# Output pieces on another queue and a longer split tail in a fused mLSTM, attention and expert layer

## The chip, the cores and the metric

The kernel is one program on one core of a Trainium2 chip. The metric is the device time of one launch in microseconds (us), the median of several runs. All data are fp32; large products are made from split operands (below).

## The reference, cut to what matters

One layer on 256 tokens of width 2048. The first half (mLSTM and a sparse attention, both fed by a wide projection of the normalised input) ends in `x = x + gate1 * y`. The change touches the start (the norm), the passage from the first half to the second, and the second half, which is a product-key expert layer:

```
h2 = rmsnorm(x, norm2_g) * (1 + scale2) + shift2
q  = (h2 @ wq).reshape(n_tok, 8, 2, 128)
sc = einsum('nhpd,pkd->nhpk', q, subkeys)        # top 16 of 128 twice, then top 16 of 256
a  = einsum('td,thkd->thk', xb, u_tab[eidx])     # 16384 experts, 2048 wide
w  = softmax(top) * gelu(a)
x  = x + gate2 * einsum('thk,thkd->td', w, v_tab[eidx])
```

## The kernel before, in words

**Split products.** A weight unit is a 128 x 1024 fp32 load of 512 KB (`load_unit`, L212, on SP's queue) into one of a ring of raw buffers (`raw_slots`). ScalarE (ACT) rounds it to a high part (L217), VectorE (DVE) subtracts to get the low part (L218). `mm3` (L242 to L244) makes a product of three matmuls: high by low, high by high, low by high. SP's queue is served in order: a load whose buffer is not yet free holds back every later issue.

**Start.** `rms_bcast` squares the input in four pieces of 128 x 1024 (L452), adds them in pairs (L453) and sums over partitions on TensorE (L455). The squares go to a ring of two buffers (`w4`), so the second pair of pieces waits until the first is used up. Behind it TensorE makes the first modulation group (L392), and only then the first projection.

**Passage to the second half.** `y_phase` makes 16 column tiles of the output projection. While the last is made, `q_first` loads the two halves of the first query tile (`wq[0]`) and splits the first half only, into the buffers hl0 and hl1. Then come the norm (L985 to L989), `make_h`, which for each of 16 blocks of 128 features runs two DVE operations of 128 x 256 (L465, L468) with one on ACT between them (L467), and the eight pieces of the residual x1, transposed on TensorE (L570), copied out of PSUM by ACT into a ring of three buffers `w2` (L1001) and stored to DRAM from ACT's queue (L1002). `peer` starts by splitting the second half of `wq[0]` into buffers of a new pool, starts seven small loads from ACT's queue (L1244 to L1254: an index row, the subkeys, an identity, four bias rows), and copies the identity on ACT (L1249). Its first loop makes 16 query tiles (two units each), and loads 20 units of the modulation `wmB`, which DVE sums up (L355, L357). Instructions up to the end of this loop are ordered by the framework, by readiness; from there on `pin()` fixes the order on each engine to the order of the code.

**U stage.** For 128 steps `e` the kernel makes expert scores (L1194, L1203, L1204). From step `G0` = 58 on, 48 steps also scatter the gates of four tokens: GpSimd and ACT make two one-hot factors (L1146 to L1148), TensorE multiplies them (L1156), ACT and DVE place the result (L1159, L1162).

**V stage.** 128 experts in 256 steps (expert e, half u of 1024 columns). Each step splits one unit of V and makes ten matmuls of 512 columns into the banks of that half (`v_mm`). The eight PSUM banks hold the whole output: quarters q = 0, 1 belong to u = 0, quarters 2, 3 to u = 1. The last `NT` = 8 experts go by halves: first u = 0 of all eight, then u = 1, so quarters 0 and 1 are complete after step 247. `v_out(q)` finishes a quarter: an ACT copy (L1391), five DVE operations (L1392 to L1397) and two stores of 256 KB (L1394, L1398), here on SP's queue. Before, `v_out(0)` stands behind step 251, `v_out(1)` behind step 252, and quarters 2 and 3 after the last step. In steps 252 to 255 only quarter 2's matmuls are made; quarter 3's follow at the end.

Of the kernel before, what the change touches and what calls it, by code (L numbers as in the profile page):

```python
# [12 lines left out]
AF = mybir.ActivationFunctionType  # L13
# [5 lines left out]
T = 256  # L19
# [3 lines left out]
TD = 192  # L23
# [3 lines left out]
C_ONE, C_MS, C_MT, C_QA, C_KA, C_CA, C_CM, C_VD = 0, 128, 256, 384, 448, 452, 454, 484  # L27
# [110 lines left out]
class Kernel:  # L138
# [307 lines left out]
    def rms_bcast(self):  # L446
        nc = self.nc
        ps = self.bank()
        for j in range(2):
            sq, s2 = self.w4(), self.w4()  # L450
            for i, t in enumerate((sq, s2)):
                nc.scalar.activation(t, self.xT[:, 8 * j + 4 * i:8 * j + 4 * i + 4, :], AF.Square)  # L452
            nc.vector.tensor_tensor(sq, sq, s2, op=ALU.add)  # L453
            for i in range(4):
                nc.tensor.matmul(ps[:, :T], self.cst[:, C_ONE:C_ONE + 128], sq[:, i * T:i * T + T], start=(j + i == 0), stop=(j == 1 and i == 3))  # L455
        r = self.wk.tile([128, T], F32, tag="rbc", name=self.nm("rbc"), bufs=1)
        nc.scalar.activation(r, ps[:, :T], AF.Sqrt, bias=self.eps, scale=1.0)
        nc.vector.reciprocal(r, r)
        return r
# [482 lines left out]
        return pc  # L942

    def q_first(self):
        self.raw_slots = self.st_raws()
        self.half_slots = [(self.st, "hl0"), (self.st, "hl1")]
        s = self.a["wq"][0].rearrange("p d c -> p (d c)")
        self.q0r = [self.load_unit(s[:, c:c + 1024]) for c in (0, 1024)]
        return self.split(self.q0r[0])

    def proj_mm(self, pc, kts):
        b = self.bank("z")
# [6 lines left out]
    def y_phase(self):  # L959
        nc = self.nc  # L960
        self.load_x()
        nxt = self.proj_load(self.a["wo"][0], (1, 0))
        self.hmix()
        kts = list(range(8, 16)) + list(range(0, 8))
        sq = self.wk.tile([128, T], F32, tag="sqs", name="sqs", bufs=1)
        for ct in range(16):
# [3 lines left out]
            pc = nxt  # L970
            nxt = self.proj_load(self.a["wo"][ct + 1], (1, 0)) if ct < 15 else self.q_first()
            b = self.proj_mm(pc, kts)
# [3 lines left out]
            else:  # L976
                s = self.w1()
# [6 lines left out]
        ps = self.bank()  # L984
        nc.tensor.matmul(ps[:, :T], self.cst[:, C_ONE:C_ONE + 128], sq, start=True, stop=False)  # L985
        nc.tensor.matmul(ps[:, :T], self.cst[:, C_ONE:C_ONE + 128], s, start=False, stop=True)
        r = self.wk.tile([128, T], F32, tag="rbc", name=self.nm("rbc"), bufs=1)
# [7 lines left out]
        for tt in range(2):  # L995
            for q in range(4):
                ps = self.bank("s")
                for j in range(4):
                    self.tr(ps[:, j * 128:j * 128 + 128], self.xT[:, 4 * q + j, tt * 128:tt * 128 + 128])
                t = self.w2()  # L1000
                nc.scalar.activation(t, ps, AF.Copy)  # L1001
                nc.scalar.dma_start(self.d_x1[tt, :, 512 * q:512 * q + 512], t)  # L1002

    def topk16(self, vals, idx, src, n):
        nc, tk = self.nc, self.tk
# [219 lines left out]
    def peer(self):  # L1225
        nc, P, a = self.nc, self.pools, self.a
# [3 lines left out]
        self.tk = tk = P.open("tk")  # L1230
        self.half_slots = [(tk, "hl0"), (tk, "hl1"), (tk, "hl2"), (gp, "ug2"), (self.st, "hl0"), (self.st, "hl1")]
        self.sc = 0
        q1 = self.split(self.q0r[1])
        self.iT = um.tile([128, 4, TD], F32, name="iT")
        self.x32 = um.tile([128, 3, KF, 64], F32, name="x32")
        self.xr = gp.tile([128, D], F32, tag="xr", name="xr", bufs=1)
# [4 lines left out]
        self.ga = gp.tile([128, 64], F32, name="ga")  # L1241
        self.sk = tk.tile([128, 2, 128], F32, name="sk")
        self.iota16 = tk.tile([128, 16], F32, name="iota16")
        nc.scalar.dma_start(self.iota16, a["idio"][:, 128:144])  # L1244
        nc.scalar.dma_start(self.sk, a["sk"])
        self.ident = tk.tile([128, 128], F32, name="ident2")
        nc.scalar.dma_start(self.ident, a["idio"][:, 0:128])
        self.idr = tk.tile([128, 128], F32R, name="idr")
        nc.scalar.activation(self.idr, self.ident, AF.Copy)  # L1249
        g2t = gp.tile([128, D], F32, tag="ug0", name="g2t", bufs=1)  # L1250
        acc, rows = [g2t[:, 0:1024]], g2t[:, 1024:1024 + T]
        bg = g2t[:, 1280:1792].rearrange("p (h c) -> p h c", h=2)
        for q in range(4):
            nc.scalar.dma_start(bg[32 * q:32 * q + 1, :, :], a["bg2"].rearrange("o (h q c) -> o q h c", h=2, q=4)[:, q])  # L1254
        self.qa = tk.tile([128, 16, T], F32, name="qa")
        self.top = tk.tile([128, 2, 8, 16], F32, name="top")
        self.isel = tk.tile([128, 2, 2, 128], F32, name="isel")
        self.WB = [wba.tile([128, 64, TD], F32, name="WBa"), None]
        nxt = self.q0 + q1
        gate2 = [f for half in range(2) for f in self.mod_gate2(half, acc, rows, bg)]  # L1260
        for i in range(16):
            for f in gate2[max(i - 2, 0) * self.GQ // 14:max(i - 1, 0) * self.GQ // 14]:
                f()
            if i == self.QX:
                self.raw_slots += [(tk, "rawx0"), (tk, "rawx1"), (gp, "ug1")]
            if i in (3, 4, 5):
                x3 = self.x32[:, i - 3]
                nc.vector.tensor_tensor(x3, *(self.hx[:, i - 3, 0:KF, k, :].bitcast(F32) for k in range(2)), op=ALU.add)
            pc = nxt
            if i < 15:  # L1270
                nxt = self.proj_load(self.a["wq"][i + 1])
            else:
                n = len(self.raw_slots)
                self.fl = [self.raw_slots[(self.uc + j) % n] for j in range(n)]
                self.ul = [(1, 0), (0, 0), (1, 1)] + [p for e in range(1, 127) for p in ((0, e), (1, e + 1))] + [(0, 127), (1, 128), (1, 129)]
                self.ur = {}
                self.last = {}
                self.pinned = len(nc.cur_bb.bb.instructions)
                for j in nc.cur_bb.bb.instructions:
                    self.last[j.engine] = j.name  # L1280
                self.u_fill()
            self.q_tile(i, pc)
# [11 lines left out]
        next(tp[0])  # L1294
        ts = list(range(24)) + [25 + i * 30 // 24 for i in range(24)]
        ge = list(range(26, 58, 2)) + [58 + i * 66 // 48 for i in range(48)]
        g4 = [e for e in range(self.G0, 128) if (e - self.G0) % 5 < 4][:TD // 4]
        dots = []
        td = 0
        k = 0  # L1300
        for e in range(128):
# [9 lines left out]
            b = self.u_mm0(e)  # L1311
# [60 lines left out]
        nv = 0  # L1372
        mm = nc.tensor.matmul
        seq = list(range(64, 128)) + list(range(64))
        NT = 8
        tail = seq[-NT:]
        order = [(e, u) for e in seq[:-NT] for u in range(2)] + [(e, u) for u in range(2) for e in tail]

# [8 lines left out]

        def v_out(q):
            c = slice(512 * q, 512 * q + 512)
            o = self.raw_tile((vx, f"o{q}"))[:, 0:512]  # L1390
            nc.scalar.activation(sh[0:64, c], y[1][q][64:128, :], AF.Copy)  # L1391
            nc.vector.tensor_tensor(o, y[0][q], g2[:, c], op=ALU.mult)  # L1392
            nc.vector.tensor_tensor(o, o, x1[:, c], op=ALU.add)
            nc.sync.dma_start(a["out"][0:128, c], o)  # L1394
            nc.vector.tensor_tensor(sh[0:64, c], y[1][q][0:64, :], sh[0:64, c], op=ALU.add)
            nc.vector.tensor_tensor(sh[:, c], sh[:, c], g2[:, c], op=ALU.mult)
            nc.vector.tensor_tensor(sh[:, c], sh[:, c], x1b[:, c], op=ALU.add)  # L1397
            nc.sync.dma_start(a["out"][128:T, c], sh[:, c])  # L1398

        late = []  # L1400
        for step, (e, u) in enumerate(order):
            if step == 128:
# [25 lines left out]
            else:  # L1428
                late.append((e, pc))
                v_mm(e, u, 0, pc)  # L1430
            if step == 251:
                v_out(0)
            if step == 252:
                v_out(1)
            self.pin()
            if e == 72 and u == 1:
                hy = self.hh.tile([128, 4, D], F32, tag="hx", name="hy", bufs=1)
# [3 lines left out]
                nc.scalar.dma_start(x1b, self.d_x1[1])  # L1441
        for e, pc in late:
            v_mm(e, 1, 1, pc)
        v_out(2)
        v_out(3)
        self.pin()

    def build(self):
# [33 lines left out]
```

## Time and profile before

| | |
|---|---|
| median of 3 runs | 2049.55 us (2049.22 to 2050.61) |
| the profiled execution | 2048.65 us, span 2046.9 us |
| mean granted clock of TensorE | 0.991 |
| TensorE (PE) busy | 1971.2 us, 96% of the span |
| DVE, ACT, GpSimd (POOL) busy | 74%, 52%, 21% |
| DMA | 612.06 MB, mean 299 GB/s |

The page also shows the span in 40 slices of 51 us. PE is busy at nine tenths or more in all but the first (7) and the last (6); its granted clock is at 9 (full) in all but the last (8). In an answer of the trace, "idle before <- releaser" in brackets is the time that the engine stood still before the instruction and what ended it. SPq and ACTq are the issue of DMAs on those engines' queues.

### The profile page before, as it was taken

Reading aid. Unit: us, or ns where it says so; the run is one execution under the profiler, and the core shown is the slowest. Engines: PE = TensorE matmul, PEld = TensorE weight load, DVE = VectorE, ACT = ScalarE, POOL = GpSimd, SP = SyncE. Lnnn points to the kernel's source line nnn. Section 1 sums busy time; section 2 is a strip of 40 time slices with the busy share of each in tenths; the row PEclk is TensorE's granted clock in tenths of the full one; section 3 lists DMA queues with packets and bytes.
Section 4 is the critical chain, followed back from the end, with each engine's and each line's share of the span. In section 5 each row is a group of like instructions: output and inputs, shape, how many; then the busy total and the mean of one; then the engine's idle time right before and its main releaser. Section 6 shows DMA issues by size and latency. Waiting matters only on the chain. (4 is left out here: it accounts for less than half of the span.)

```text
span 2046.9 us, 34175 instructions
## 1 busy us (share of the span) xinstructions
PE 1971.2 (96%) x12601; PEld 1707.9 (83%) x12601; DVE 1522.9 (74%) x2695; ACT 1062.3 (52%) x2055; POOL 426.1 (21%) x359
## 2 busy tenths in 40 slices
PE   7999999999998999999999999999999999999996
PEld 6887877675898999999999999999677777777774
DVE  3777778864557669989966666676788888888885
ACT  5444336673445434333377778763455555555552
POOL 0000001001010000011166667651122221322200
PEclk9999999999999999999999999999999999999998
DMA  8877986619886878788888988888999999999972
GB/s 328 306 276 271 330 317 247 227 48 361 280 291 227 292 252 283 245 316 305 304 302 318 331 316 311 327 316 294 362 338 366 341 361 342 396 348 357 365 278 86
DMA packets 151544, 612.06 MB, mean 299 GB/s; under 512 B 17089, under 2 KB 18257, under 8 KB 134609
## 3 DMA queue, kind: packets, MB, share of 16 engines
q1 hardware_dynamic: 130320, 469.25, 64.3%
q0 software_dynamic: 18432, 134.23, 17.2%
q10 hardware_dynamic: 2624, 6.40, 0.8%
q8 instruction: 100, 1.64, 0.3%
q14 instruction: 68, 0.55, 0.1%
HBM read 605.61 MB, written 4.20 MB: 298 GB/s over the span
## 5 line engine op out<-in xcount | busy, mean ns | idle before, releaser
L217 ACT ACTIVATE hl<-raw 128x512 fp32r<-128x512 f32 (+1 forms) x601 | 483.9, 815 | 553.9 <-PE z L244 242.2
L218 DVE TENSOR_TENSOR hl<-raw,hl 128x512 fp32r<-128x512 f32 (+1 forms) x601 | 542.3, 921 | 235.3 <-ACT hl L217 234.0
L1194 PE MATMUL z<-x,raw 128*128 128x192 f32 x2048 | 353.9, 326 | 0.0
L1194 PEld LDWEIGHTS z<-x,raw 128*128 128x128 f32 x2048 | 336.9, 190 | 0.4 <-PE t L1022 0.4
L1204 PE MATMUL z<-hx 128*128 128x384 f32 x976 | 289.5, 361 | 0.0
L1203 PE MATMUL z<-hx 128*128 128x192 f32 x976 | 258.4, 265 | 0.8 <-DVE hx L218 0.8
L242 PE MATMUL z<-hx,hl 128*128 128x256 f32 x848 | 244.3, 288 | 12.0 <-DVE hx L468 10.0
L244 PE MATMUL z<-hx,hl 128*128 128x256 f32 x848 | 241.7, 286 | 2.7 <-DVE hl L218 2.6
L243 PE MATMUL z<-hx,hl 128*128 128x256 f32 x848 | 241.5, 285 | 0.0
L1093 POOL DMA_INDIRECT ug<-in_V_dram,gix x64 | 131.9, 2061 | 427.8 <-DVE yg L1116 368.5
L1203 PEld LDWEIGHTS z<-hx 128*128 128x128 f32 x976 | 186.5, 191 | 3.1 <-DVE hx L218 2.4
L1093 POOL DMA_INDIRECT ug<-in_UG_dram,gix x64 | 92.7, 1448 | 440.0 <-DVE ts L1061 249.1
L1204 PEld LDWEIGHTS z<-hx 128*128 128x128 f32 x976 | 183.5, 188 | 0.0
L242 PEld LDWEIGHTS z<-hx,hl 128*128 128x128 f32 x848 | 163.3, 193 | 23.3 <-ACT hl L217 9.3
L1146 POOL TENSOR_SCALAR e<-iota,iT 128x128 f32<-128x128 f32 x192 | 166.0, 877 | 75.2 <-PE t L1156 61.0
L218 DVE TENSOR_TENSOR hx<-raw,hx 128x1024 fp32r<-128x1024 f32 x124 | 151.4, 1221 | 25.5 <-ACT hx L217 25.5
L244 PEld LDWEIGHTS z<-hx,hl 128*128 128x128 f32 x848 | 163.0, 192 | 5.1 <-DVE hl L218 4.5
L243 PEld LDWEIGHTS z<-hx,hl 128*128 128x128 f32 x848 | 163.1, 192 | 0.3
L1116 DVE SCALAR_TENSOR_TENSOR yg<-ug,gw,yg 128x2048 f32<-128x2048 f32 x63 | 147.8, 2346 | 0.6 <-DMA ug<-in_V_dram,gix 0.6
L1208 ACT ACTIVATE c<-z 128x192 f32<-128x192 f32 x128 | 41.9, 327 | 202.6 <-PE z L1204 189.3
L1103 DVE SCALAR_TENSOR_TENSOR ug<-ug,xr 128x2048 f32<-128x2048 f32 x64 | 146.8, 2294 | 0.0
L217 ACT ACTIVATE hx<-raw 128x1024 fp32r<-128x1024 f32 x124 | 130.0, 1049 | 0.0
(384 smaller groups left out, 3615.7 us busy)
## 6 DMA issues: line engine op xcount, KB each, us to landing
raw<-in_U_dram SPq DMA_DIRECT2D x256, 512.0 KB
raw<-in_V_dram SPq DMA_DIRECT2D x256, 512.0 KB
raw<-in_wmB_dram SPq DMA_DIRECT2D x128, 512.0 KB
raw<-in_wt_dram SPq DMA_DIRECT2D x64, 512.0 KB
raw<-in_wmA_dram SPq DMA_DIRECT2D x48, 512.0 KB
raw<-in_wo_dram SPq DMA_DIRECT2D x32, 512.0 KB
raw<-in_wq_dram SPq DMA_DIRECT2D x32, 512.0 KB
raw<-in_wz_dram SPq DMA_DIRECT2D x30, 512.0 KB
```

What stands on the lines that cost most here:

```text
L217: nc.scalar.activation(hi, raw, AF.Copy)
L218: nc.vector.tensor_tensor(lo, raw, hi.bitcast(F32), op=ALU.subtract)
L242: mm(ps, sh, ml, start=first, stop=False, skip_group_check=skip)
L243: mm(ps, sh, mh, start=False, stop=False, skip_group_check=skip)
L244: mm(ps, sl, mh, start=False, stop=last, skip_group_check=skip)
L1093: self.nc.gpsimd.indirect_dma_start(out=t, out_offset=None, in_=self.a[name].rearrange("a b d -> (a b) d"), in_offset=bass.IndirectOffsetO ...
L1103: nc.vector.scalar_tensor_tensor(t, t, 1.0, self.xr, op0=ALU.mult, op1=ALU.mult, accum_out=self.ga[:, n:n + 1])
L1116: nc.vector.scalar_tensor_tensor(self.yg, t, w, self.yg, op0=ALU.mult, op1=ALU.add)
L1146: nc.gpsimd.tensor_scalar(e0, self.iota, self.iT[:, 0, t:t + 1], None, op0=ALU.is_equal)
L1194: self.nc.tensor.matmul(b[:, 0:TD], r[:, dt * 128:dt * 128 + 128], self.x32[:, :, dt, :], start=dt == 0, stop=False, skip_group_check=True)
L1203: mm(b[:, TD:2 * TD], lo[:, c], self.hx[:, 0:3, dt, 0, :], start=False, stop=False, skip_group_check=True)
L1204: mm(b[:, 0:2 * TD], hi[:, c], self.hx[:, 0:3, dt, :, :].rearrange("p b k t -> p k b t"), start=False, stop=dt == 15, skip_group_check=True)
```

## The change

Six edits. (1) `rms_bcast` squares into four separate places (of `zqk`, free at that time). (2) `q_first` loads and splits both halves of `wq[0]`; its four split pieces lie in hl0, hl1 and two of the five raw buffers, and the query loop begins with a ring of eight raw buffers in another order. (3) The x1 pieces are copied to eight separate places in `zqk` and stored from SP's queue. (4) The seven small loads of `peer` move to query tile 3, the copy of the identity to tile 8. (5) The gate scatters begin at U step 59. (6) `NT` = 12; `v_out` gives up control after each piece; its first ten pieces (quarters 0 and 1) stand one per step behind steps 245 to 254, and their stores are issued from GpSimd's queue.

```diff
 rms_bcast:
-            sq, s2 = self.w4(), self.w4()
+            sq, s2 = (self.zqk[:, 8 * j + 4 * i:8 * j + 4 * i + 4, :] for i in range(2))
 q_first:
-        self.raw_slots = self.st_raws()
-        self.half_slots = [(self.st, "hl0"), (self.st, "hl1")]
-        s = self.a["wq"][0].rearrange("p d c -> p (d c)")
-        self.q0r = [self.load_unit(s[:, c:c + 1024]) for c in (0, 1024)]
-        return self.split(self.q0r[0])
+        r = self.st_raws()
+        self.half_slots = [(self.st, "hl0"), (self.st, "hl1"), r[2], r[3]]
+        self.raw_slots = [r[0], r[1], r[4]]
+        self.sc = 0
+        pc = self.proj_load(self.a["wq"][0])
+        self.q_raws = [r[4], r[0], r[1], r[2], r[3]]
+        return pc
 y_phase:
-                t = self.w2()
-                nc.scalar.activation(t, ps, AF.Copy)
-                nc.scalar.dma_start(self.d_x1[tt, :, 512 * q:512 * q + 512], t)
+                t = self.zqk[:, 8 * tt + 2 * q:8 * tt + 2 * q + 2, :]
+                nc.scalar.activation(t, ps.rearrange("p (a b) -> p a b", a=2), AF.Copy)
+                nc.sync.dma_start(self.d_x1[tt, :, 512 * q:512 * q + 512], t.rearrange("p a b -> p (a b)"))
 peer:
-        q1 = self.split(self.q0r[1])
+        self.raw_slots = [self.q_raws[0], (tk, "rawx0"), (tk, "rawx1"), (gp, "ug1")] + self.q_raws[1:]
+        self.uc = 0
...
-        nxt = self.q0 + q1
+        nxt = self.q0
...
-            if i == self.QX:
-                self.raw_slots += [(tk, "rawx0"), (tk, "rawx1"), (gp, "ug1")]
+            if i == 3:
+                nc.scalar.dma_start(self.iota16, a["idio"][:, 128:144])
+                nc.scalar.dma_start(self.sk, a["sk"])
+                nc.scalar.dma_start(self.ident, a["idio"][:, 0:128])
+                for q in range(4):
+                    nc.scalar.dma_start(bg[32 * q:32 * q + 1, :, :], a["bg2"].rearrange("o (h q c) -> o q h c", h=2, q=4)[:, q])
+            if i == 8:
+                nc.scalar.activation(self.idr, self.ident, AF.Copy)
...
-        g4 = [e for e in range(self.G0, 128) if (e - self.G0) % 5 < 4][:TD // 4]
+        g4 = [e for e in range(self.G0 + 1, 128) if (e - self.G0 - 1) % 5 < 4][:TD // 4]
...
-        NT = 8
+        NT = 12
...
         def v_out(q):
-            o = self.raw_tile((vx, f"o{q}"))[:, 0:512]
+            o = ob[:, c]
+            q_eng = nc.gpsimd if q < 2 else nc.sync
             nc.scalar.activation(sh[0:64, c], y[1][q][64:128, :], AF.Copy)
             nc.vector.tensor_tensor(o, y[0][q], g2[:, c], op=ALU.mult)
+            yield
             nc.vector.tensor_tensor(o, o, x1[:, c], op=ALU.add)
-            nc.sync.dma_start(a["out"][0:128, c], o)
+            q_eng.dma_start(a["out"][0:128, c], o)
+            yield
             nc.vector.tensor_tensor(sh[0:64, c], y[1][q][0:64, :], sh[0:64, c], op=ALU.add)
+            yield
             nc.vector.tensor_tensor(sh[:, c], sh[:, c], g2[:, c], op=ALU.mult)
+            yield
             nc.vector.tensor_tensor(sh[:, c], sh[:, c], x1b[:, c], op=ALU.add)
-            nc.sync.dma_start(a["out"][128:T, c], sh[:, c])
-
+            q_eng.dma_start(a["out"][128:T, c], sh[:, c])
+            yield
+
+        outs = (None for q in range(4) for _ in v_out(q))
...
-            if step == 251:
-                v_out(0)
-            if step == 252:
-                v_out(1)
+            if 245 <= step < 255:
+                next(outs)
...
-        v_out(2)
-        v_out(3)
+        for _ in outs:
+            pass
```

The seven small loads and the identity's copy are taken out of the place where `peer` had them.

## Rows read from the trace of the kernel before

**Rows 1.** The waits of PE: who waited for whom, us in total, times, longest.

```profile
PE z L1384 <- ACT hl L217: 12.5, 3, 7.3
PE t L455 <- DVE w L453: 11.3, 2, 11.1
PE z L242 <- DVE hx L468: 10.0, 3, 4.7
...
PE t L1156 <- DVE WBb L1162: 2.3, 4, 0.7
```

**Rows 2.** Timeline of PE at the end: start us, us, instruction, idle before.

```profile
2002.71 0.39 PE L242 MATMUL z<-hl,wh 128*128 128x512 f32 x1
...
2015.86 0.40 PE L244 MATMUL z<-hl,wl 128*128 128x512 f32 x1
2019.35 0.51 PE L1384 MATMUL z<-hl,wh 128*128 128x512 f32 x1 [3.09 <-ACT hl L217]
...
2029.86 0.80 PE L1384 MATMUL z<-hl,wh 128*128 128x512 f32 x1 [7.28 <-ACT hl L217]
...
2039.93 0.40 PE L244 MATMUL z<-hl,wl 128*128 128x512 f32 x1
```

**Rows 3.** Busy time by window at the end; the number behind POOL is PEclk.

```profile
2020.00:2034.00 14.00, 5.65 (x13) 3.37 (x14) 7.03 (x9) 3.17 (x3) 0.00 (x0) 0.51 0.46 150
```

**Rows 4.** Timeline of ACT at the end.

```profile
2018.24 1.06 ACT L217 ACTIVATE hl<-raw 128x1024 fp32r<-128x1024 f32 x1 [9.49 <-DMA raw<-in_V_dram]
```

**Rows 5.** Timeline of SP's queue at the end.

```profile
1962.40 31.19 SPq L212 DMA_DIRECT2D raw<-in_V_dram  x15
2010.74 0.35 SPq L1394 DMA_DIRECT2D out_dram<-raw  x1
...
2013.22 0.38 SPq L212 DMA_DIRECT2D raw<-in_V_dram  x1
...
2024.39 1.58 SPq L212 DMA_DIRECT2D raw<-in_V_dram  x3
```

**Rows 6.** Groups by line from 1990 us on: busy us, mean ns of one, idle.

```profile
L218 DVE TENSOR_TENSOR hl<-raw,hl 128x1024 fp32r<-128x1024 f32 x13 | 15.9, 1225 | 21.5 <-ACT hl L217 21.4
L217 ACT ACTIVATE hl<-raw 128x1024 fp32r<-128x1024 f32 x12 | 12.7, 1060 | 28.7 <-DMA raw<-in_V_dram 19.8 <-PE s L244 9.0
L1393 DVE TENSOR_TENSOR raw<-raw,hy 128x512 f32<-128x512 f32 x4 | 2.8, 693 | 0.1
```

**Rows 7.** Costliest groups of the whole page: the gathers of V and their sum.

```profile
L1093 POOL DMA_INDIRECT ug<-in_V_dram,gix x64 | 131.9, 2061 | 427.8 <-DVE yg L1116 368.5
...
L1116 DVE SCALAR_TENSOR_TENSOR yg<-ug,gw,yg 128x2048 f32<-128x2048 f32 x63 | 147.8, 2346 | 0.6 <-DMA ug<-in_V_dram,gix 0.6
```

**Rows 8.** The chain that ended last, a piece at the start of V.

```profile
1440.02 35.93 DMA ug<-in_V_dram,gix x4
```

**Rows 9.** Timeline of PE in the passage to the query tiles.

```profile
630.57 0.41 PE L242 MATMUL z<-hx,hl 128*128 128x256 f32 x1 [2.26 <-DVE hx L468]
...
641.26 0.58 PE L242 MATMUL z<-hx,hl 128*128 128x256 f32 x1 [4.65 <-DVE hx L468]
...
646.12 0.38 PE L242 MATMUL z<-hx,hl 128*128 128x256 f32 x1 [0.16 <-ACT hl L217]
```

**Rows 10.** Timeline of ACT and its queue in the same passage.

```profile
640.58 0.63 ACT L217 ACTIVATE hl<-raw 128x512 fp32r<-128x512 f32 x1
...
642.34 2.41 ACTq L1254 DMA_DIRECT2D g2t<-in_bg_dram  x3
...
645.43 2.20 ACT L217 ACTIVATE hl<-raw 128x512 fp32r<-128x512 f32 x4 [0.33 <-issue]
```

**Rows 11.** Timeline of DVE in the same passage.

```profile
639.54 1.67 DVE L468 SCALAR_TENSOR_TENSOR hx<-m,modc,hx 128x256 fp32r<-128x256 f32 x4
...
642.45 1.89 DVE L1268 TENSOR_TENSOR x<-hx 128x512 f32<-128x512 f32 x3
```

**Rows 12.** Timeline of SP's queue in the same passage.

```profile
643.43 0.33 SPq L212 DMA_DIRECT2D raw<-in_wq_dram  x1
```

More of the change, by code (lines that the diff above doesn't have):

```diff
@@ L454, in rms_bcast @@
             for i in range(4):
-                nc.tensor.matmul(ps[:, :T], self.cst[:, C_ONE:C_ONE + 128], sq[:, i * T:i * T + T], start=(j + i == 0), stop=(j == 1 and i == 3))
+                nc.tensor.matmul(ps[:, :T], self.cst[:, C_ONE:C_ONE + 128], sq[:, i, :], start=(j + i == 0), stop=(j == 1 and i == 3))
         r = self.wk.tile([128, T], F32, tag="rbc", name=self.nm("rbc"), bufs=1)
@@ L1243, in peer @@
         self.iota16 = tk.tile([128, 16], F32, name="iota16")
-        nc.scalar.dma_start(self.iota16, a["idio"][:, 128:144])
-        nc.scalar.dma_start(self.sk, a["sk"])
         self.ident = tk.tile([128, 128], F32, name="ident2")
-        nc.scalar.dma_start(self.ident, a["idio"][:, 0:128])
         self.idr = tk.tile([128, 128], F32R, name="idr")
-        nc.scalar.activation(self.idr, self.ident, AF.Copy)
         g2t = gp.tile([128, D], F32, tag="ug0", name="g2t", bufs=1)
@@ L1252, in peer @@
         bg = g2t[:, 1280:1792].rearrange("p (h c) -> p h c", h=2)
-        for q in range(4):
-            nc.scalar.dma_start(bg[32 * q:32 * q + 1, :, :], a["bg2"].rearrange("o (h q c) -> o q h c", h=2, q=4)[:, q])
         self.qa = tk.tile([128, 16, T], F32, name="qa")
```

## The prediction

> **What bounds the kernel now.** I read the page first: TensorE is busy in 96% of the span at a granted clock of 0.991, so time can only come from the places where it stands still or runs slowly. The waits of PE give those places [rows 1]: its longest wait is for the split of V (L1384 behind ACT's L217, 12.5 us in three waits), then the start (L455, 11.3 us, of which 11.1 is the first load), then the first query tile (L242 behind L468, 10.0 us), and far behind them the gate scatters (L1156, 2.3 us). Two of the three V waits lie in the last 30 us.
>
> There, PE's timeline shows matmuls at a regular distance up to 2015.86, then waits of 3.09 and 7.28 us, and the last matmul at 2039.93 [rows 2]. ACT, whose split PE waits for, had itself waited 9.49 us for a load [rows 4]. SP's queue says why the load was late [rows 5]: its last run of loads ended at 1962.40 + 31.19 = 1993.59; the next thing it issued was a store of `v_out(0)` at 2010.74, and only behind that, at 2013.22, the next load. So 17 us of SP's time went into waiting for the data of a store, with loads behind it whose buffers came free one every 2.3 us. The same happened behind `v_out(1)`: the last three loads left at 2024.39. The bound at the end is the order of one queue; neither TensorE nor the memory is.
>
> **The change part by part.** *The end (edit 6).* From 2002.71 to 2015.86 lie 57 matmuls, 0.231 us each. Behind 2015.86, 40 matmuls remain (four units' first halves and four second halves of five each). Without a stall the last starts at 2015.86 + 40 x 0.231 = 2025.09 in place of 2039.93: 14.8 us. Of these, 3.09 + 7.28 are the waits shown, the rest shorter waits and matmuls at the lower level: the granted clock is 0.51 from 2020 to 2034 [rows 3], about 1.2 of 2.4 GHz, behind the idle stretches. The steps by which it goes: with the stores gone from SP, the four loads leave at one per step from about 1996 on and, at the 5.0 us from 2013.22 to 2018.24 [rows 4, 5], land by about 2008, before ACT's regular splits ask for them (about 2009 to 2016).
>
> What takes the place of the old `v_out` must fit into steps of 2.31 us. On DVE a step has a split of 1.23 and one piece of 0.69 [rows 6]: 1.92. On ACT a split of 1.06 and at most one copy, smaller than a split: under 2.12. Four more experts by halves put their weights into every step instead of every second one, but add none. In the first four of these steps DVE also sums gathers, 2.35 each [rows 7], about one per 3.6 steps (64 gathers in 230 steps): with some 0.5 for the weights (an estimate from two subtractions smaller than the 0.69 piece), 1.23 + 0.5 + 0.65 = 2.4 against 2.31. That is 0.4 us too much over four steps, and the splits run up to three units (7 us) ahead, so I cost it at nothing; without this lead it would cost its 0.4. GpSimd issues four stores; its nearest row is the V gather, 2.06 us of GpSimd each [rows 7], and it has no other work once the 64 gathers are out. Gathers of four times a store's bytes took 9.0 us each when they shared the memory with loads [rows 8]; the last of the four stores leaves at about 2016, some 16 us before the new end. Both are hidden; without that cover, 9 us at most. The path behind the last matmul is as before: quarter 3's five DVE operations and its stores. Bounds: 14.8 at best; 10.8 if one wait like the first stays (its 3.1 plus about 0.9 of slow matmuls). I take 14.8, since the buffers and the transfers are there.
>
> *The first query tile (edits 2, 3, 4).* PE waits 4.65 us until 641.26, in the middle of this tile [rows 9]. The releaser is named as `make_h`, but ACT's split of the second half of `wq[0]` runs at 640.58, behind all of `make_h` [rows 10], and its result fits 641.26 better. With both halves split during the last output tile, PE follows DVE's `make_h`: the last four low parts are written from 639.54 to 641.21 [rows 11], and their twelve matmuls, at about 0.2 us each for the lower clock, end near 642.5. The tile's second half ends at 646.12 now [rows 9]: up to 3.6 us. Then the second tile's splits come at 645.43, because ACT first works through the seven small loads (three took 2.41 us) [rows 10]; moved away, ACT can split at 641 and DVE at about 641.2, and the 0.16 wait goes too. Against it: DVE may first do the three additions of 1.89 us [rows 11]; the second tile's first low part is then written near 643.8 (641.2 + 1.89 + 0.7), which leaves about 2.3. The x1 stores cost SP eight issues of 0.35 (2.8 us); SP has time for them, since its next load left only at 643.43 [rows 12]. I read that time as a load into space that the last x1 stores still occupied; from `zqk` they no longer do, so loads can run ahead as far as before. The seven small loads at tile 3 block ACT for about 7 x 0.8 = 5.6 us there; six split pieces ahead cover about that. Range -2 to 3.8 (3.6 + 0.16) (the loss: SP's loads held behind x1 stores); I take 3.0, near the row that has the splits early.
>
> *The start (edit 1).* PE has only 0.2 us of waits at L455 beyond the first 11.1 [rows 1]. Four places let the second squares run early, but TensorE's work from there on is the same. A raw buffer now comes free later, as L392 stands behind all of L455. Range -0.6 to 0.8, taken 0.2.
>
> *The scatters (edit 5).* All waits there sum to 2.3 us in four [rows 1]; a step's shift may drop or add two of them: -1.2 to 1.2, taken 0.3 for more time before the first.
>
> **The sum.** 14.8 + 3.0 + 0.2 + 0.3 = 18.3 us. Against the profiled execution, 2048.65 (span 2046.9, 1.75 around it), that is 2030.35; this execution lies 0.9 below the median of 2049.55, so the median after is 2031.2.
>
> **Rivals.** *The passage gives nothing.* The small loads or stores on SP take what the early split brings, or the query tiles, which need two units each and 20 of `wmB`, wait for transfers 3 us later. For: SP is in order, and the next load waited until 643.43 [rows 12]. Against: no byte is added, and the eight buffers are the same. Time: 2049.55 - 14.8 to 2049.55 - 14.8 + 2, 2034.7 to 2036.7.
>
> *Only the issue time is saved.* The loads at the end wait for something else as well, and four issues of 0.35 us leave SP: 1.4 us. With the rest, 1.4 + 3.5 = 4.9, so 2044.6. Against it stand 17 us between two issues of SP, with loads waiting [rows 5]. The Trainium skill, "DMA: Bandwidth & Descriptors", section "Rules for kernel authors", has this rule: spreading DMAs over SP, ACT and GpSimd "only saves sequencer issue time". By that rule alone the end would be worth 1.4 us; the rows speak against it here, as the queue stood blocked by a store's wait and not by its issue.
>
> *Slower: the seven small loads in the query loop.* If each of them on ACT's queue waits for an earlier big transfer, 5.0 us by the landing above, ACT stands 35 us at tile 3. Two half pieces last 4.9 us there (641.26 to 646.12 [rows 9]), so a lead of five covers some 12. The remaining 23 us exceed the 18.3 gained: 2049.55 + 23 - 18.3 = 2054. It decides from a wait of (12 + 18.3) / 7 = 4.3 us each. For: they stand in the middle of a stage with many transfers. Against: three of them took 2.41 us, with transfers under way [rows 10].
>
> *No change.* The gain at the end is taken back at the same place, as quarters 2 and 3 or the splits become late on DVE: 2049.5. Against: 1.92 of 2.31 us per step.
>
> **How the numbers follow.** Forecast 0.72; the passage gives nothing 0.15; only issue time 0.05; slower 0.03; no change 0.03; more than 20.6 (all upper bounds: 14.8 + 3.8 + 0.8 + 1.2) 0.02. About 0.2%, 4.1 us, is what a measurement of this kernel can tell from no change. The forecast, the passage, issue time and the rest above it are faster by more: 0.72 + 0.15 + 0.05 + 0.02 = 0.94; same 0.03; slower 0.03. The range begins at the sum of the upper bounds, 2028.9, with a little below it, 2028.0, and takes in the passage's 2036.7: 2037.0.
>
> **What would show it.** End: SP's loads leave every 2.3 us up to the last; no wait of PE over 1 us behind step 240; PEclk full; the four early stores on GpSimd. Passage: the second half of the first query tile starts without a gap of 4 us and ACT's next splits come near 641. The forecast is wrong if PE still waits for ACT's split in the last four units, if the query tiles show new waits of several us around tile 3, or if the V stage waits for weights at the first tail steps.

## The result, and the profile after

The changed kernel takes 2029.43 us (median of 6 runs, 2027.63 to 2035.00) against 2049.39 for the kernel before (6 runs, 2044.99 to 2050.61): a ratio of 0.9905, 95% interval 0.9891 to 0.9919. 20.0 us are gone. The profiled execution took 2029.15 us, its span is 2027.4; PE is busy 97% of it. (The ratios are estimated from all runs, so they can differ a little from the quotient of two medians.) Lines behind 940 have moved by up to ten (L1384 is L1387 now, L985 is L987, L1015 is L1017, L1420 is L1430).

The waits of PE after, as in [rows 1]: engine, line, who it waited for, us in total, times, longest.

```profile
PE t L455 <- DVE zqk L453: 11.1, 1, 11.1
...
PE z L242 <- DVE hx L468: 5.2, 4, 3.0
...
PE s L1387 <- ACT hl L217: 2.4, 1, 2.4
PE z L242 <- ACT hl L217: 2.4, 3, 1.0
PE t L1158 <- DVE WBb L1164: 2.2, 4, 0.6
...
PE z L1387 <- ACT hl L217: 1.2, 2, 0.8
```

The wait for the split of V (L1387, listed under two tiles) fell from 12.5 us to 3.6. What is left stands early in the V stage, from 1468 to 1480 us, where the kernel before waited 2.1; the 10.4 us of the last 30 are gone. L242 behind L468 fell from 10.0 to 5.2. The wait of 0.2 at the second squares is gone.

**The end.** SP's queue from 1969 us on, as [rows 5]:

```profile
1969.90 28.01 SPq L212 DMA_DIRECT2D raw<-in_V_dram  x13
2017.45 0.34 SPq L1399 DMA_DIRECT2D out_dram<-hy  x1
```

The first and the last of the four early stores in GpSimd's timeline:

```profile
1994.79 0.61 POOL L1399 DMA_DIRECT2D out_dram<-hy  x1 [45.74 <-DVE hy L1398]
...
2012.30 0.54 POOL L1406 DMA_DIRECT2D out_dram<-sh  x1 [6.38 <-DVE sh L1405]
```

The busy time by window, as [rows 3]: width, busy time and count of PE, PEld, DVE, ACT and POOL, then PEclk:

```profile
2010.00:2020.00 10.00, 10.00 (x45) 7.64 (x44) 6.42 (x8) 1.88 (x4) 0.54 (x1) 1.00 0.14 52
```

The last matmul in PE's timeline, as [rows 2]:

```profile
2020.18 0.40 PE L244 MATMUL z<-hl,wl 128*128 128x512 f32 x1
```

The last 13 loads leave in one run, one per 2.3 us on average, up to 1997.9; no store stands among them. PE is busy through 2010 to 2020 at a granted clock of 1.00, where it was busy 40% of 2020 to 2034 at 0.51 before. GpSimd stands 45.74 us idle before its first store, and nobody waits for it.

**A ruler that scatters less.** Total times of one kernel differ by several us between executions, and so do the positions of its stages. Distances inside a stage repeat far better (about 1 us). I use two. The *end distance* runs from ACT's copy ahead of step 238 to the end of the span. That copy in ACT's timeline of the kernel before:

```profile
1975.86 1.92 ACT L1420 ACTIVATE sh<-yg 64x2048 f32<-64x2048 f32 x1
```

And in that of the changed kernel:

```profile
1970.95 1.92 ACT L1430 ACTIVATE sh<-yg 64x2048 f32<-64x2048 f32 x1
```

Before it is 2046.9 - 1975.86 = 71.0 us, after 2027.4 - 1970.95 = 56.4: 14.6 us. The *query distance* runs from the norm's reciprocal on DVE to ACT's copy of a query tile. Its zero in DVE's timeline, in the kernel before and in the changed one:

```profile
626.66 1.75 DVE L989 RECIPROCAL rbc<-rbc 128x256 f32<-128x256 f32 x1 [0.99 <-ACT rbc L988]
...
627.76 1.75 DVE L991 RECIPROCAL rbc<-rbc 128x256 f32<-128x256 f32 x1 [0.88 <-ACT rbc L990]
```

The 16 copies in the answer for their line, before and after: durations in ns, then the first and the last start:

```profile
L1015 ACT ACTIVATE qa<-z x16: 363/385/385, 647.5 to 735.9; 128x256 f32<-128x256 f32 x16
...
L1017 ACT ACTIVATE qa<-z x16: 363/385/387, 644.0 to 731.5; 128x256 f32<-128x256 f32 x16
```

To tile 15 it is 103.8 us after and 109.2 before (735.9 - 626.66): 5.4 us. Together 20.0 us, as much as the medians differ; the two profiled spans differ by 19.5, as the stages between these distances shifted by 0.5. All kernels of this study, in us (tiles count from 0; copies read from each trace's ACT timeline). The runs were taken on several occasions: beside sp_behind, qfirst_old, x1_act and small_front the kernel before took 2050.8 us, beside the others 2049.1 to 2049.4, so medians of different rows compare to about 2 us at best.

| kernel | what differs | tile 0 | tile 2 | tile 8 | tile 15 | end distance | median |
|---|---|---|---|---|---|---|---|
| before | | 20.9 | 31.7 | 66.4 | 109.2 | 71.0 | 2049.39 |
| after | | 16.2 | 29.0 | 63.2 | 103.8 | 56.4 | 2029.43 |
| after_again | the same kernel | 15.5 | 28.2 | 62.5 | 103.0 | 56.4 | 2028.74 |
| tail_only | before + edit 6 | 20.9 | 31.7 | 66.1 | 109.0 | 56.4 | 2037.15 |
| no_tail | after - edit 6 | 15.9 | 29.0 | 63.3 | 103.8 | 71.2 | 2043.38 |
| pieces_sp | early stores on SP | 15.5 | 28.9 | 63.1 | 103.7 | 77.6 | 2049.36 |
| whole_gpsimd | no pieces, NT = 8, raw buffers | 16.2 | 29.1 | 63.3 | 103.9 | 57.5 | 2029.35 |
| sp_behind | early stores on SP, last | 15.5 | 28.2 | 62.5 | 103.0 | 55.9 | 2027.17 |
| qfirst_old | edit 2 undone | 21.1 | 32.4 | 66.8 | 107.7 | 56.4 | 2035.38 |
| x1_act | x1 stores on ACT | 17.5 | 32.1 | 66.4 | 109.5 | 56.4 | 2030.40 |
| small_front | edit 4 undone | 22.7 | 35.8 | 70.0 | 110.5 | 56.1 | 2032.81 |
| loads_front | small loads in front | 20.8 | 32.8 | 68.8 | 111.8 | 56.4 | 2035.62 |
| split_only | edits 3, 4 undone | 25.0 | 36.1 | 70.9 | 116.1 | 56.4 | 2039.23 |
| late_rows | other order of the end | 15.5 | 28.3 | 62.6 | 103.1 | 54.4 | 2025.77 |

### The profile page after: what moved, and what is told of

The parts are those of the page before. It is cut to its first block, busy times and chain, and to the rows that moved or that the text cites. A ratio compares the mean times of both kernels' runs of the same rounds, so it can differ in the third digit from the quotient of the medians.

```text
span 2027.4 us, 34161 instructions
## 1 busy us (share of the span) xinstructions
PE 1967.6 (97%) x12601; PEld 1706.9 (84%) x12601; DVE 1523.3 (75%) x2695; ACT 1061.9 (52%) x2054; POOL 437.2 (22%) x363
## 3 DMA queue, kind: packets, MB, share of 16 engines
q0 software_dynamic: 18752, 135.27, 17.5%
## 4 chain that ended last, share of the span: by engine, by line
PE 83%; DVE 8%; DMA 5%; ACT 3%; issue 1%; ACTq 0%; SPq 0%; DVEq 0%
PE z L1196 13%; PE z L242 9%; PE z L244 9%; PE z L243 9%; PE z L1206 9%; PE z L1205 4%; PE m L339 2%; DMA raw<-in_wt_dram 2%; PE t L1158 2%; DVE hl L218 2%; PE z L1388 1%; PE o L243 1%; PE t L1388 1%; PE s L1388 1%; PE m L1388 1%; PE s L243 1%
## 5 line engine op out<-in xcount | busy, mean ns | idle before, releaser
L242 PE MATMUL z<-hx,hl 128*128 128x256 f32 x848 | 245.2, 289 | 8.0 <-DVE hx L468 5.2
L1095 POOL DMA_INDIRECT ug<-in_V_dram,gix x64 | 136.8, 2138 | 422.6 <-DVE yg L1118 373.4
L1095 POOL DMA_INDIRECT ug<-in_UG_dram,gix x64 | 97.2, 1519 | 431.9 <-DMA raw<-in_U_dram 243.3
L242 PEld LDWEIGHTS z<-hx,hl 128*128 128x128 f32 x848 | 163.5, 193 | 20.1 <-DVE hx L468 6.8
```

The lines of the kernel that those rows point to most:

```text
L242: mm(ps, sh, ml, start=first, stop=False, skip_group_check=skip)
L1095: self.nc.gpsimd.indirect_dma_start(out=t, out_offset=None, in_=self.a[name].rearrange("a b d -> (a b) d"), in_offset=bass.IndirectOffsetO ...
```

## The experiments

**Each half alone: tail_only and no_tail.** The first is the kernel before with edit 6, the second the changed kernel with the V stage of before.

> The kernel before with edit 6 alone (NT = 12, pieces one per step, quarters 0 and 1 stored from GpSimd's queue). Theory (the end is bound by the order of SP's queue; the edit removes two stores of it that stood 17 us in front of waiting loads): the tail gives 14.7 us and nothing else moves, so 2049.4 - 14.7 = 2034.7, with 1.5 us either way for the scatter of the runs; SP's last loads leave in one unbroken run, and no wait of PE over 1 us is left behind step 240. Rival (only the issue of four stores leaves SP): 4 x 0.35 = 1.4 us, 2048.0, with the 7 us wait of PE still there.

> The changed kernel with the V stage of before (edits 1 to 5 without edit 6). Theory: the passage and the start give what the trace of the changed kernel shows ahead of the tail, 4.9 us at step 240 (1977.8 against 1972.9), so 2049.4 - 4.9 = 2044.5, with 1.5 us either way; PE's waits of about 3 and 7 us come back at the end. Rival (edits 1 to 5 do nothing by themselves, the earlier position in that one trace is scatter between executions): 2049.4.

tail_only: 2037.15 us (4 runs, 2033.16 to 2039.32), 0.9933 of before (0.9913 to 0.9952). no_tail: 2043.38 (7 runs), 0.997 (0.9958 to 0.9982). Both gain, as the theory has it, and the end distance says 56.4 and 71.2: edit 6 is worth 14.6 to 14.8 us, and edits 1 to 5 move the end by 0.2 at most. In no_tail PE waits 3.00 and 7.69 us in the last 30 us again, in tail_only not at all in the last 60. The total of tail_only is 2.5 us above my figure; in its trace step 238 comes at 1981.15, 5 us later than before, and 4.5 of these are there at the norm's reciprocal already (631.11), in stages that the edit does not touch. Edits 1 to 5 are worth 5.7 us by the total, 5.4 by the query distance.

**The queue or the pieces: pieces_sp, whole_gpsimd, sp_behind.**

```diff
 pieces_sp
-            q_eng = nc.gpsimd if q < 2 else nc.sync
+            q_eng = nc.sync
 whole_gpsimd (and v_out without its yields)
-        NT = 12
+        NT = 8
...
-            o = ob[:, c]
+            o = self.raw_tile((vx, f"o{q}"))[:, 0:512]
...
-            if 245 <= step < 255:
-                next(outs)
+            if step == 251:
+                v_out(0)
+            if step == 252:
+                v_out(1)
 sp_behind
-            q_eng = nc.gpsimd if q < 2 else nc.sync
+            post = (lambda *x: held.append(x)) if q < 2 else nc.sync.dma_start
...
+        for x in held:
+            nc.sync.dma_start(*x)
         for e, pc in late:
```

> The changed kernel with the four early stores on SP's queue again, the pieces still one per step. Theory (a store that waits for DVE blocks the loads behind it): each store stands in SP's order at its step, and the loads behind it leave only when DVE has made its piece, so SP loses its lead of about four units; the loads then take 5 us to land against 2.3 us per step, and PE waits again: I expect 3 to 10 us lost, 2032 to 2039, SP's issue at the end broken by gaps of several us ahead of each store. Rival (it is the pieces, spread one per step, that save the end; the queue doesn't matter): no change, 2029.4 within 1.

> The changed kernel with NT = 8 and the two early outputs whole, behind steps 251 and 252 as before, in raw buffers as before, but with their stores on GpSimd's queue. Theory (the queue's order is the cause): SP's loads no longer stand behind a store in order; what remains is DVE's two bursts of five operations (3.5 us each) between the splits, and two raw buffers held until the stores have landed, so 1 to 5 us above the changed kernel, 2030 to 2035. Rival (the pieces one per step are needed, since the bursts make the splits late): 8 us or more above it, over 2037.

> The changed kernel with the four early stores back on SP's queue, but issued there only behind the last load of V. Theory (what counts is that no store stands ahead of a waiting load in one queue; GpSimd is only one way to get that): as the changed kernel, from the sum over the gathers (its copy on ACT, step 238) to the end 56.4 us, 2029.4 in all, within 1.5. Rival (the stores must go out early from a queue of their own, else six stores of 256 KB crowd at the end): 3 us or more longer behind step 238, over 2032.

pieces_sp: 2049.36 us (10 runs), 0.9996 of before (0.9984 to 1.0008). The whole gain is gone: the end distance, 77.6, is 6.6 us worse than before, which takes back what edits 1 to 5 keep (tile 15 still comes at 103.7). I had expected a loss of 3 to 10 us; it is 20. Its SP queue:

```profile
1991.82 0.34 SPq L1399 DMA_DIRECT2D out_dram<-hy  x1
1992.25 1.34 SPq L212 DMA_DIRECT2D raw<-in_V_dram  x3
2002.62 0.34 SPq L1406 DMA_DIRECT2D out_dram<-sh  x1
2003.05 0.87 SPq L212 DMA_DIRECT2D raw<-in_V_dram  x2
2012.64 0.34 SPq L1399 DMA_DIRECT2D out_dram<-hy  x1
```

Its DVE between the stores:

```profile
1996.96 1.23 DVE L218 TENSOR_TENSOR hl<-raw,hl 128x1024 fp32r<-128x1024 f32 x1 [5.18 <-ACT hl L217]
1998.11 0.68 DVE L1401 TENSOR_TENSOR sh<-s,sh 64x512 f32<-64x512 f32 x1
...
2001.90 0.69 DVE L1405 TENSOR_TENSOR sh<-sh,hy 128x512 f32<-128x512 f32 x1
2009.05 1.23 DVE L218 TENSOR_TENSOR hl<-raw,hl 128x1024 fp32r<-128x1024 f32 x1 [6.46 <-ACT hl L217]
```

This is a circle, and it explains the size. A store waits for its piece on DVE (L1405 ends at 2002.59, the store leaves at 2002.62). The piece stands on DVE behind the splits of the earlier steps. Such a split waits for a load (5.18 and 6.46 us idle). And the load stands on SP behind the store. So once the lead is used up each store costs a whole landing: the four of them stand 10 to 12 us apart (1991.82 to 2024.89), some 5 us more each than in the changed kernel (4.6 to 6.9 us apart), and the loads issued at 2003.05 and 2013.40 reach ACT's split 4.9 and 5.1 us later (2007.96 and 2018.48).

whole_gpsimd: 2029.35 us (4 runs), 0.9899 (0.9882 to 0.9915), end distance 57.5: 1.1 us above the changed kernel. It differs from no_tail only in the queue of the four early stores, and the end distances are 57.5 and 71.2: the queue is worth 13.7 us. The pieces, their own buffers and the four more experts are worth about that 1.1 (one wait of PE, 0.82 us at 2017.22, is left in whole_gpsimd). sp_behind: 2027.17 us (4 runs), 0.9891 (0.9871 to 0.9910), end distance 55.9. It moves no store to another queue; its SP queue:

```profile
1970.66 27.85 SPq L212 DMA_DIRECT2D raw<-in_V_dram  x13
1998.56 0.42 SPq L1452 DMA_DIRECT2D out_dram<-hy  x1
2001.08 0.34 SPq L1452 DMA_DIRECT2D out_dram<-sh  x1
...
2012.54 0.33 SPq L1452 DMA_DIRECT2D out_dram<-sh  x1
```

The rival that the stores need a queue of their own falls. What counts is that no store that waits stands ahead of a load. The rule from the Trainium skill that I named ("DMA: Bandwidth & Descriptors", section "Rules for kernel authors"), by which spreading DMAs over the engines for bandwidth "only saves sequencer issue time", would leave 1.4 us here, and whole_gpsimd gave 13.7; the measurement decides. sp_behind, which spreads nothing and does as well, shows that the gain is not bandwidth either: what counted was the order in one queue, 20 us between pieces_sp and after for four waiting stores.

**Which edit makes the passage faster: qfirst_old, small_front, x1_act.** Each undoes one of edits 2, 4 and the queue of edit 3. (In small_front the copy of the identity stands behind the four bias rows, in the kernel before ahead of them in the code.)

```diff
 qfirst_old (as in the kernel before)
...
-        pc = self.proj_load(self.a["wq"][0])
...
+        return self.split(self.q0r[0])
...
 small_front (the seven loads and the copy, ahead of the query loop)
+        nc.scalar.dma_start(self.iota16, a["idio"][:, 128:144])
...
+        nc.scalar.activation(self.idr, self.ident, AF.Copy)
 x1_act
-                nc.sync.dma_start(self.d_x1[tt, :, 512 * q:512 * q + 512], t.rearrange("p a b -> p (a b)"))
+                nc.scalar.dma_start(self.d_x1[tt, :, 512 * q:512 * q + 512], t.rearrange("p a b -> p (a b)"))
```

> The changed kernel with edit 2 undone: only the first half of the first query tile is split ahead, and the raw buffers of the query stage are grouped as before. The measure is the distance from the reciprocal of the norm in the passage to the copies of the query tiles: 109.2 us to the last tile before, 103.8 after; at tile 2 31.7 and 29.0. Theory (the split ahead gives the 2.7 us at tile 2, the other grouping the 2 us at tile 10, where a split stood behind a late wmB piece on DVE): both come back, 108 to 110 us to the last tile, about 5 us more in all, 2034.5. Rival (the x1 copies without the ring of three, edit 3, give the gain): 104 to 105 us, no change in all. In between: 31.7 at tile 2 and no step at tile 10, 106.5 us, when the small loads' place (edit 4) and not the grouping took the late wait away.

> The changed kernel with edit 4 undone: the seven small loads and the copy of the identity stand ahead of the query loop again. Theory (three of these loads took ACT 2.4 us before, but the first tile's weights are split ahead, so ACT has the time of two tile halves for them): 103.8 to 105 us from the reciprocal to the last query tile, 0 to 1.2 us in all. Rival (the small loads are what held ACT's splits of the second tile): tile 1 at 26 us in place of 23.9 and 2 us or more kept to the last tile, 106 us, 2031.5.

> The changed kernel with the eight x1 stores issued from ACT's queue in place of SP's. Theory (eight issues of about 0.35 us, 2.8 us, on an engine that stands idle 1.07 us in each group of three blocks of the norm): no change at the first query tiles beyond 1 us, 103.8 to 105 us to the last one, 2029.4 to 2030.5. Rival (ACT is what paces the passage, so the issues lengthen it): 2.8 us more at tile 0, 2032. Other rival (SP's next loads left at 641 because of the stores that it had to issue; without these the loads run ahead): up to 1 us less.

Measured to tile 15: 107.7, 110.5 and 109.5 us. For qfirst_old neither the theory (108 to 110) nor the rival (104 to 105) came, but nearly the case that I had put between them: 3.9 us back, with tile 2's part lost (32.4) and no step at tile 10, so the grouping was not what removed that. For the other two my theory fell: I had them at 1.2 us or less, and each loses 5.7 us or more. Each edit undone alone takes back most of the gain or all of it. The traces show the same pattern thrice: PE waits for a split on ACT, and ACT's split stands behind something in its order. The wait in PE's timeline of qfirst_old:

```profile
640.61 0.58 PE L242 MATMUL z<-hx,hl 128*128 128x256 f32 x1 [4.80 <-ACT hl L217]
```

There it is the second half of tile 0, whose splits stand behind the norm's work on ACT, as before. In small_front PE waits 5.89 us for the same line at 647.31; PE, then ACT and its queue ahead of that:

```profile
647.31 0.58 PE L242 MATMUL z<-hx,hl 128*128 128x256 f32 x1 [5.89 <-ACT hl L217]
...
641.04 3.02 ACTq L1256 DMA_DIRECT2D g2t<-in_bg_dram  x4
646.43 0.31 ACT L1257 ACTIVATE idr<-ident 128x128 fp32r<-128x128 f32 x1 [6.33 <-DMA ident<-in_idio_dram]
646.64 2.17 ACT L217 ACTIVATE hl<-raw 128x512 fp32r<-128x512 f32 x4
```

The copy of the identity waits 6.33 us for its load, and the splits stand behind it. In x1_act PE waits 1.87 us at 643.74; PE, then ACT and its queue:

```profile
643.74 0.38 PE L242 MATMUL z<-hx,hl 128*128 128x256 f32 x1 [1.87 <-ACT hl L217]
...
640.60 2.41 ACTq L1266 DMA_DIRECT2D g2t<-in_bg_dram  x3
643.06 1.15 ACT L217 ACTIVATE hl<-raw 128x512 fp32r<-128x512 f32 x2 [2.90 <-DMA g2t<-in_bg_dram]
```

In x1_act the framework, which orders by readiness, put small loads ahead of the first splits of tile 1, though the code has them at tile 3; after, they came behind these (643.98 and later). Totals: qfirst_old 2035.38 us, 0.9936 of before (0.9916 to 0.9956); small_front 2032.81, 0.9922 (0.9902 to 0.9942); x1_act 2030.40, 0.9907 (0.9887 to 0.9928). For x1_act the total loses 1.0 us where the distance loses 5.7; in its trace the stretch from tile 15 to the copy ahead of step 238 took 1236.9 us, in the traces with all of edits 1 to 5 1237.6 to 1239.9, so 0.7 to 3.0 us may come back there. With 4 runs and stages that shift by several us that stays open.

**What of edit 4: loads_front, and edit 2 without the others: split_only.** The first has the seven loads in front and the copy at tile 8; the second is small_front with the x1 copies of before (ring of three, ACT's queue).

```diff
 loads_front
-            if i == 3:
-                nc.scalar.dma_start(self.iota16, a["idio"][:, 128:144])
...
+        nc.scalar.dma_start(self.iota16, a["idio"][:, 128:144])
 split_only (small_front, and)
-                t = self.zqk[:, 8 * tt + 2 * q:8 * tt + 2 * q + 2, :]
+                t = self.w2()
...
```

> The changed kernel with the seven small loads ahead of the query loop as before, but the copy of the identity on ACT still at query tile 8. With both ahead the last query tile came at 110.5 us behind the reciprocal in place of 103.8, and PE waited 5.9 us for a split on ACT that stood behind this copy, which had waited 6.3 us for its load. Theory (ACT is in order: the copy's wait for its load holds the splits, not the loads' issue): with the copy at tile 8 the distance is 104 to 106 us and that wait is 2 us at most. Rival (the issue of the seven loads, 4.3 us of ACT's queue at the wrong moment, holds the splits): 108 us or more, with a wait of 3 us or more at the second tile.

> The changed kernel with edits 3 and 4 undone and edit 2 kept: the first query tile is split ahead, but the x1 copies go through the ring of three and are stored from ACT's queue, and the small loads and the identity's copy stand ahead of the loop. Edits 2, 3 and 4 each undone alone have cost 3.9, 5.7 and 6.7 us of the distance from the reciprocal to the last query tile (103.8 us changed, 109.2 before). Theory (the three only work together, since ACT's and SP's queues are in order and each place holds the splits again): 109 us or more, no gain over before from edit 2 alone; 2034.5 to 2036 in all. Rival (the edits add up, about 2 us each): 106 to 107.5 us.

loads_front: 2035.62 us (6 runs), 0.9932 (0.9918 to 0.9946). To tile 2 it is 32.8 us, between small_front's 35.8 and the changed kernel's 29.0: the waiting copy was worth 3.0 of the 6.8 us, the loads' issue 3.8. My theory, that the copy alone held the splits, falls: PE's wait at the second tile is still 3.92 us. On ACT's queue the seven issues fill 638.12 to 643.15, and the splits come behind; the last line is PE's:

```profile
639.57 3.58 ACTq L1256 DMA_DIRECT2D g2t<-in_bg_dram  x4
643.19 2.19 ACT L217 ACTIVATE hl<-raw 128x512 fp32r<-128x512 f32 x4 [4.56 <-DMA sk<-in_sk_dram]
...
643.87 0.38 PE L242 MATMUL z<-hx,hl 128*128 128x256 f32 x1 [3.92 <-ACT hl L217]
```

Its distance then grows from tile 2 to 15 by 4 us more than small_front's or the changed kernel's. Most of that is a step at tiles 8 and 10, and the kernel before has such a step too, at tile 10, 2.0 us. There a split stands on DVE behind a piece of the modulation (L357) that waits for its load. DVE of the kernel before:

```profile
703.05 1.28 DVE L357 SCALAR_TENSOR_TENSOR g2t<-raw,csl,g2t 128x1024 f32<-128x1024 f32 x1 [2.95 <-DMA raw<-in_wmB_dram]
704.25 3.09 DVE L218 TENSOR_TENSOR hl<-raw,hl 128x512 fp32r<-128x512 f32 x5
```

And its PE:

```profile
705.00 0.39 PE L244 MATMUL z<-hx,hl 128*128 128x256 f32 x1 [1.70 <-DVE hl L218]
```

The step comes and goes with edits that move the order ahead of it (tiles 9 and 13 in x1_act); I made no experiment on it alone. split_only: 116.1 us to tile 15 and 2039.23 us in all (6 runs), 0.9944 (0.9930 to 0.9957). Edit 2 without 3 and 4 is not only no gain: its passage is 6.9 us slower than before. ACT stands 6.63 us behind its small loads, and PE waits 4.5 us for a low part (at 649.75) that stands on DVE behind a piece of the modulation (L355, at 648.34).

**A version that beats both: late_rows.** The last four units make y[1] of both quarters within the steps; y[0] follows, and DVE works through quarter 2's and 3's second token half meanwhile.

```diff
-                v_mm(e, u, 0, pc)
+                for hf in range(2):
+                    v_mm(e, u, hf, pc, 1)
...
-        for e, pc in late:
-            v_mm(e, 1, 1, pc)
-        for _ in outs:
-            pass
+        for hf in range(2):
+            for e, pc in late:
+                v_mm(e, 1, hf, pc, 0)
+        for q in (2, 3):
+            v_sh(q)
+        for q in (2, 3):
+            v_o(q)
```

> A version meant to beat the changed kernel: in the last four units PE makes the matmuls of the second token half (y[1], two each) for both quarters in the steps, and the 24 matmuls of the first token half (y[0]) behind them, so that of the five DVE operations of quarter 3 only two stand behind the last matmul. Theory (the path at the end is the last matmul, then DVE's operations of 0.7 us each, then the landing of the last store): three operations less, 2.1 us, of which some 0.2 to 0.7 is lost as DVE has eight operations, 5.6 us, to do in the 5.5 us of these 24 matmuls: from the copy of step 238 to the end 54.5 to 55 us in place of 56.4, and 1.4 to 1.9 us less in all. Rival (with four in place of five matmuls in each of the last steps PE reaches the last splits too early and waits, or the landing of the stores sets the end): 56 us or more, no gain.

> The changed kernel once more, beside the three others on the same chip, as the measure for effects of one or two microseconds: 2029.4 within 1.5, 103.8 us from the reciprocal to the last query tile and 56.4 us from the copy of step 238 to the end, each within 1 (theory: these two distances repeat where the total scatters by several us). Rival: the distances scatter as much as the total, and then they decide nothing about the edits undone one by one.

late_rows: 2025.77 us (4 runs, 2023.23 to 2028.12), 0.9881 of before (0.9865 to 0.9897); after_again on the same chip 2028.74 (4 runs, 2026.87 to 2030.33), 0.9894. End distances 54.4 and 56.4: 2.0 us, as the theory has it; the intervals of the totals overlap. From the last matmul's start to the end it is 5.2 us (2023.6 - 2018.36) in place of 7.2 (2027.4 - 2020.18), since DVE is done 1.98 us (at 2020.34) and not 3.90 us (at 2024.08) behind it. The end of its DVE timeline:

```profile
2018.93 0.68 DVE L1423 TENSOR_TENSOR hy<-z,hy 128x512 f32<-128x512 f32 x1
2019.65 0.69 DVE L1424 TENSOR_TENSOR hy<-hy 128x512 f32<-128x512 f32 x1
```

The two distances of after_again repeat within 0.8 us (103.0 for 103.8; 56.4 both), so they decide where the totals don't.

## Why the prediction was right, and where not

**The time.** 2031.2 was forecast, 2029.4 came, 1.8 less; the gain was 20.0 us where the sum had 18.3. The six runs lie between 2027.63 and 2035.00, so that the median came this near is partly luck; the terms below are checked one by one.

**The end, 14.8.** From the copy ahead of step 238 to the last matmul's start it was 64.07 us before (2039.93 - 1975.86) and is 49.23 after (2020.18 - 1970.95): 14.84. The count of matmuls at their regular distance was exact. Of it 14.6 reach the end: the last matmul stands 7.2 us before it in place of 7.0. The step that names the cause, loads behind a store that waits, is shown by whole_gpsimd against no_tail (another queue and nothing else, 13.7 us), by pieces_sp (one line, 20 us) and by sp_behind. What took the old order's place was covered as said: no wait of PE over 0.3 us in the last 60 us, and the stores took GpSimd 0.54 to 0.61 us each, where I had allowed 2.06.

**The passage, 3.0 (bound 3.8).** It gave 5.4, above the bound. To tile 2 it is 2.7 (31.7 to 29.0), so the term that I worked out was about right there, though not in its steps: tile 0 came 4.7 us earlier, and 2.0 of them were lost at tile 1 (25.9 to 23.9). What I left out lies behind it: the wait of 1.70 us at 705.00 stands in the trace of before, and I had read that stage only up to its second tile. It makes 2.0 us at tile 10; the rest comes in steps of a few tenths. Two reasons of mine were weak. I put the seven small loads at tile 3 and priced them there; the framework issued them from 643.98 on, in the first tiles, where ACT's next split (646.71) stood 2.35 us behind them. And I wrote as if the early split gave the gain and the other two edits only cost or kept something: undone one by one, each takes back 3.9 us or more.

**The start, 0.2.** It gave nothing or a little less: the caveat that raw buffers come free later came true. The new wait stands ahead of the last modulation matmuls, in PE's timeline of the changed kernel:

```profile
21.10 0.65 PE L392 MATMUL m<-raw,cs 128*32 128x128 f32 x16 [0.90 <-DMA raw<-in_wmS_dram]
...
25.50 0.39 PE L242 MATMUL z<-hx,hl 128*128 128x256 f32 x1 [3.03 <-DVE hx L468]
```

Over the traces with edit 1 it is 0.7 to 1.5 us. The first projection starts at 25.50, against 25.36 before. No run took edit 1 alone.

**The scatters, 0.3.** The four waits sum to 2.2 us in place of 2.3, and one at the first half of the factors fell from 0.6 to 0.2: about 0.5, as sized. No run took edit 5 alone.

**The rivals.** "Only the issue time" (2044.6) is refuted by tail_only and whole_gpsimd. "The passage gives nothing" is refuted by no_tail, and "no change" by the result: no split came late on DVE at the end. "Slower, as the small loads hold ACT" did not happen, and none of the traces shows 5 us for each load; but that small loads hold ACT's splits is real: in loads_front by the 5.0 us that seven issues take, in small_front by the copy's wait as well (6.7 us in the passage). Its chance of 0.03 rested on three loads that took 2.41 us; that the place of seven loads could cost this much was in the timeline of ACT's queue, had I asked what else stands behind them.

## What to carry to other kernels

In an engine or queue that works in order, ask of each instruction that waits what stands behind it: four stores of 256 KB that waited for their data cost 20 us here, as loads stood behind them and the data stood behind the splits of such loads. Moving the stores to an idle queue or behind the last load served alike (end distances of 56.4 and 55.9), and splitting the work around them was worth little (1.1). Edits that clear one queue may be worth nothing one by one, since the next blocker in the order takes over (edit 2 without 3 and 4 made the passage 6.9 us slower; 3 and 4 were not run without the others); test them together and undone singly, and measure by distances inside a stage when the totals scatter by more than the effect.

## What the runs showed that I had not expected

A store of 256 KB issued by GpSimd held that engine 0.54 to 0.61 us, a quarter to three tenths of a gather's issue (2.06 us, [rows 7]). Seven small loads fill ACT's queue for 5.0 us (638.12 to 643.15 in loads_front), and ACT's next split stood 4.56 us behind them. The stages of one kernel shift by several us from execution to execution: the copy ahead of step 238 stands between 1968.2 and 1974.6 us in the seven traces whose first five edits are those of the changed kernel, while both distances of these repeat within about 1 us where the end is the same.
